# Queries and keys with both halves of the input side by side, and two value weight splits moved to the head of the norm

## The chip, the cores and the metric

The kernel runs on one core of one Trainium2 chip. The metric is the device time of one execution in microseconds (us). Times of several runs are given as their median. One execution was taken with the hardware profiler; its rows are what the prediction is read from.

## The reference

Two blocks of a transformer work on 256 tokens of width 1024. The change lies in the first block's attention layer and in the normalization ahead of it:

```python
h = modulate(rmsnorm(x, norm_mix[1]), sh1, sc1)
qkv = h @ w_qkv                     # (256, 1024) @ (1024, 3072)
q, k, v = split(qkv, 3)             # 16 heads of 64
logits = q @ k.T * 64**-0.5 + bias  # causal, one block of 256 keys
o = softmax(logits) @ v
x = x + g1 * (o @ w_o)
```

Ahead of it stands the first MLP (`relu(h @ w_up)**2 @ w_down`, width 4096), behind it the second MLP of the block, and then a second block with a gated delta rule, a forgetting attention and a gated MLP.

## The kernel before

All inputs are 32-bit floats, and TensorE takes each operand as a high part and a low part (32-bit floats of reduced precision): a product is the sum of three matmuls, high by high, low by high and high by low (`mm3`). Weights come from DRAM in loads of 1 MB (128 x 2048), issued on SP's queue into three raw buffers. Each load holds two pieces of 1024 columns. A piece is split when it is first asked for (`Chunk.piece`): ScalarE writes the high part (L248), VectorE subtracts it from the raw weights for the low part (L254). Five buffers hold the high parts of pieces, five the low parts.

The down projection of the MLP (`rows_steps`, tiles `dn`) sums into four banks, one for each half of the tokens (t) and of the columns (n). Its last chunk ends with token half 0; the matmuls of token half 1 are held back and handed to the next boundary. Ahead of the last chunk `prefetch` asks for the first pieces of the next weights, here four pieces of the value weights (`wv`).

A boundary (`boundary`) adds the sums to x (`add`: times the gate, L547, then to x, L548), squares and sums each row on ScalarE (L346), works out the row's factor (L354 to L323), normalizes (`xn`; VectorE L595 the first 512 columns, ScalarE L596 the rest), transposes on PE (L599), scales and shifts on ScalarE (`hf`, L392) and splits the result into high and low on VectorE (L398, L399). Inside a boundary the instructions of PE, VectorE and ScalarE keep the order in which they are written; `products(n)` puts n steps of the held matmuls, and then of the first products of the next layer, between them. The branch taken ahead of attention is the last one (`else`): seven steps, the transposes of half 0, one step, four, two, the transposes of half 1, two. The same branch is taken by the boundary "f" ahead of the last MLP. Outside a boundary a list scheduler orders what each engine does, after the order of the program, the buffers and its own estimate of times.

Attention takes the values of the first 512 columns (tiles `v`), and then the projections of q and k (tiles `qk`), in an order on PE that is written out: for each half of the heads, q and k of four heads, then q and k of the next four (`project`, two tiles of 128 rows by 256 tokens in each call; 16 tiles in all). Scores, transposes of the probabilities and their products with the values are put between the steps by a table of due times; each projection step counts 0.64 there. The projections use the two banks of the kind `mm`, and so do the value tiles. `ride` puts leftover work of other layers (column sums `wmc`, L473, on VectorE) behind a projection; it may start after the instruction of VectorE named in `ride_after`.

The MLP of the second layer and the gated MLP of the second block keep the high and the low part of their input side by side in one buffer (`hl_beside`), so that one matmul of 512 columns streams both over the high weights (L1010), and one of 256 streams the high part over the low weights (L1011); ScalarE copies one half of the bank (L1017) and VectorE adds the other (L1018). They use four banks, `mm` and `tp` in turn (`halves_tile`).

Of the kernel before, what the change touches and what calls it, by code (L numbers as in the profile page):

```python
# [12 lines left out]
ALU = mybir.AluOpType  # L13

P = 128
# [121 lines left out]
def costing(gen, cost):  # L137

    for _ in gen:
        yield cost  # L140
# [20 lines left out]
def build(tc, a, out):  # L161
# [4 lines left out]
    with ctx:  # L166
# [13 lines left out]
        def mm_tile(name):  # L180
            return pmm.tile([P, 512], F32, tag="mm", name=name)
# [16 lines left out]
        def last_on(engine):  # L198
            return next(i for i in reversed(nc.cur_bb.bb.instructions) if i.engine == engine)
# [81 lines left out]
        def vcol(v):  # L281
            return vecs[:, v * KT:(v + 1) * KT]
# [139 lines left out]
        def hl_tiles(name, n):  # L422
            hi = big_tile(f"{name}_hi", F32R)[:, :KT * n].rearrange("p (k n) -> p k n", k=KT)
            lo = big_tile(f"{name}_lo", F32R)[:, :KT * n].rearrange("p (k n) -> p k n", k=KT)
            return hi, lo
# [128 lines left out]
        def boundary(ac, gate, scale, shift, h, c0, name, ahead, final=None):  # L554
# [3 lines left out]
            with tc.manual_schedule(engines=VA | {mybir.EngineType.PE}):  # L558
# [9 lines left out]
                def add(t, n):  # L568
                    c = slice(n * 512, (n + 1) * 512)
                    add_to_x(ac[t, n], t, n, gate, None, f"{name}{t}{n}")  # L570
                    if final is not None:
                        vec.tensor_tensor(src[t][:, c], x[:, t, c], final[:, c], ALU.mult)
# [34 lines left out]
                def products(n):  # L607
                    for _ in range(n):
                        next(ahead[0], None)

                add(0, 0)
                squares(0, 0)
                add(0, 1)
                squares(0, 1)
                w = ahead[1]
                if final is not None:
                    products(R_REST + 1)
                    normalize(0)
                    products(5)
                    w.piece_hi(3)  # L620
                    add(1, 0)
                    hfs = [scaled(0, kt) for kt in (0, 2)]
                    squares(1, 0)
                    add(1, 1)
                    squares(1, 1)
                    split(hfs[0], 0, 0)
                    split(hfs[1], 0, 2)
                    hfs = [scaled(0, kt) for kt in (4, 6)]
                    products(4)

                    def beside():
                        w.piece_lo(3)
                        products(2)

                    normalize(1, beside)
                    split(hfs[0], 0, 4)
                    split(hfs[1], 0, 6)
                    products(4)
                elif w is not None:
                    products(R_HOLD)  # L640
                    w.piece_hi(2)
                    normalize(0)
                    products(8 - R_HOLD)
                    w.piece_lo(2)
                    for kt in range(0, KT, 2):
                        split(scaled(0, kt), 0, kt)
                    w.piece_hi(3)
                    add(1, 0)
                    squares(1, 0)
                    add(1, 1)  # L650
                    squares(1, 1)
                    w.piece_lo(3)
                    products(6)
                    normalize(1)
                    products(2)
                else:
                    products(R_REST - 1)
                    normalize(0)
                    products(1)
                    add(1, 0)  # L660
                    hfs = [scaled(0, kt) for kt in (0, 2)]
                    squares(1, 0)
                    split(hfs[0], 0, 0)
                    split(hfs[1], 0, 2)
                    products(4)
                    add(1, 1)
                    hfs = [scaled(0, kt) for kt in (4, 6)]
                    squares(1, 1)
                    split(hfs[0], 0, 4)
                    products(2)  # L670
                    normalize(1, lambda: split(hfs[1], 0, 6))
                    products(2)
# [320 lines left out]
        def ws_steps(w, h, ft, ps, c0=0, n=S, grain=4):  # L993

            for kt in range(KT):
                mm3(ps, w(ft * PIECE + kt * P, P), hl(h, kt, slice(c0, c0 + n)), kt == 0, kt == KT - 1)
                if (kt + 1) % grain == 0:
                    yield
# [3 lines left out]
                pass  # L1002

        def ws_halves(w, h, ft, ps):


            p2 = ps.rearrange("p (e n) -> p e n", e=2)
            for kt in range(KT):
                wl = w(ft * PIECE + kt * P, P)
                pe.matmul(p2, wl[0], both(h, kt, slice(0, S)), start=kt == 0, stop=False)  # L1010
                pe.matmul(p2[:, 0], wl[1], h[0][:, kt], start=False, stop=kt == KT - 1)  # L1011

        def halves_tile(q, name):
            return (mm_tile, tp_tile)[q](name)
# [63 lines left out]
        def prefetch(w, n=4):  # L1078
            def go():
                for i in range(n):  # L1080
                    w.piece(i)
            return go

        def mlp(i, h, w0, wn, at, ahead=None):
# [73 lines left out]
            def chunk(j):  # L1158
                at(j)
                nxt = max(j + 1, len(acts)) if j != 1 or i else 0  # L1160
                if nxt < 8 and nxt not in acts:
# [2 lines left out]

            return drain(rows_steps(8, chunk, lambda j, k, t: (acts[j][:, 0, k, t * P:(t + 1) * P],
                                                               acts[j][:, 1, k, t * P:(t + 1) * P]),
                                    f"dn{i}", prefetch(wn, (4, 3)[i]), hold=True))


        def softmax_rows(ps, bias, n, name, p=None):  # L1170
# [30 lines left out]
        def attention(i, h, w0, wn):  # L1201
# [31 lines left out]

            def project(w, half, which, pr):
                dst, sc = ((qT, 0.125), (kT, 1.0))[which]
                ps = mm_tile(f"qk{which}{half}{pr}")
                for q in range(2):
                    yield from costing(ws_steps(w, h, 2 * pr + q, ps[:, q * S:(q + 1) * S], grain=2), 0.64)
                kt = 4 * half + 2 * pr
                o4 = dst[:, kt:kt + 2].rearrange("p k (t n) -> p (k t) n", t=2)  # L1240
                p4 = ps.rearrange("p (a n) -> p a n", n=P)
                ride_after[:] = [last_on(mybir.EngineType.DVE)]
                act.activation(o4, p4[:, :, ::-1] if which == 0 else p4, AF.Copy, scale=sc)
                riding()

            def riding():
# [151 lines left out]

        wv0 = split_chunk(a["w_v"][0], "wv0")
        ac, rest = mlp(0, mlp0_h, None, wv0, lambda j: rel_bias_vector() if j == 1 else None, wu02)  # L1400
        h = hl_tiles("att1", S)
        firsts = []

        def ahead(rest, w, h, name):
# [2 lines left out]
            firsts.append(mm_tile(name))  # L1407
            yield from tm_steps(w, h, 0, P, firsts[-1], 1)

        boundary(ac, lambda: gates[0, 1], *mods(1, 0), h, 0, "att1", (ahead(rest, wv0, h, "v00"), None))  # L1410
        wu1 = Chunk(a["w_up0"], "wu10", inmraw=2)
        ac, rest = attention(1, h, wv0, wu1)
        while len(pending) > 4:
            ride(4)
        h = hl_beside("mlp1", S)
        boundary(ac, lambda: gates[1, 0], *mods(1, 1), h, 0, "mlp1", (ahead(rest, wu1, h, "up100"), wu1))

        def wide_row(src, name):
            row = big_tile(name)[:, :D]
# [33 lines left out]
            yield from meta  # L1453
            yield from first

        boundary(ac, lambda: gates[1, 1], vcol(V_ATT), None, u, NMETA, "u", (second_ahead(), wfv), early["nf"])
        p1ctx.close()
        p2 = ctx.enter_context(tc.tile_pool(name="p2", bufs=1, reuse_waits="tile"))
        masks = p2.tile([P, M_N], F32, name="masks")
# [580 lines left out]
        ac, rest = drain(wo)  # L2040

        fh = hl_beside("f", S)
        boundary(ac, None, vcol(V_FFN), None, fh, 0, "f", (ahead(rest, wg0, fh, "gu00"), None))
        NJ = DFF2 // 256

        def fa_tile(j):
# [160 lines left out]
```

## Time and profile before

| | |
|---|---|
| time, median of 3 runs | 926.99 us (925.73 to 929.45) |
| time of the profiled execution | 926.48 us |
| its span, first to last instruction | 924.7 us |
| PE busy | 902.5 us, 98% |
| VectorE (DVE) busy | 664.6 us, 72% |
| ScalarE (ACT) busy | 521.1 us, 56% |
| mean granted TensorE clock | 0.995 of full speed |

The span is shorter than the time by what lies before the first and behind the last instruction. Busy times are sums over the whole span; an engine with 72% can be full in one stage and half idle in another. Matmuls overlap, so the length of one says less than the distance from one start to the next.

### The profile page before, as it was taken

The page shows a single profiled execution, that of the slowest core. Times are in us where ns is not written, and L with a number is a line of the kernel's source. Part 1 is how long each engine was busy: PE and PEld are TensorE (multiplying, and loading weights), DVE is VectorE, ACT ScalarE, POOL GpSimd, SP SyncE. Part 2 cuts the span into 40 slices and gives each one's busy share as a digit, 9 for nine tenths or more (in the row PEclk, how much of TensorE's full clock was granted, in tenths as well). Part 3 has the DMA queues.
Part 4 walks back from the last instruction along what each step waited for, and adds up shares of the span by engine and source line. Part 5 has one row for each costly group of instructions (what it writes and reads, how often), then busy time and mean ns, then how long its engine had stood idle before and what let it go on. Part 6 is the DMA issues. An engine that isn't in the chain of part 4 may idle for free.

```text
span 924.7 us, 14385 instructions
## 1 busy us (share of the span) xinstructions
PE 902.5 (98%) x5501; PEld 763.3 (83%) x5501; DVE 664.6 (72%) x1296; ACT 521.1 (56%) x957; POOL 12.7 (1%) x22
## 2 busy tenths in 40 slices
PE   7999999999899999999999999999999999999996
PEld 3668889999799987888888878999988788888885
DVE  1686889998698785896566678797458775666554
ACT  4466544445467764665555656766456555545552
POOL 0000000000000000000000001000000000000000
PEclk9999999999999999999999999999999999999998
DMA  9998879999477561875565634432113565555531
GB/s 363 420 421 325 302 279 373 378 342 354 139 252 285 171 229 42 295 277 183 190 219 181 241 110 173 138 110 75 46 47 98 199 204 204 184 182 183 186 134 45
DMA packets 34552, 198.25 MB, mean 214 GB/s; under 512 B 4186, under 2 KB 6818, under 8 KB 14002
## 3 DMA queue, kind: packets, MB, share of 16 engines
q1 hardware_dynamic: 34338, 197.27, 59.5%
q8 instruction: 43, 0.70, 0.3%
q14 instruction: 25, 0.20, 0.1%
q10 hardware_dynamic: 146, 0.08, 0.0%
HBM read 196.24 MB, written 1.09 MB: 213 GB/s over the span
## 4 chain that ended last, share of the span: by engine, by line
PE 88%; DVE 4%; DMA 3%; issue 2%; ACT 1%; SPq 0%; POOL 0%; DVEq 0%; POOLq 0%; ACTq 0%
PE gu L1010 8%; PE dn L265 6%; PE dn L266 6%; PE dn L267 6%; PE up L1010 6%; PE gu L1011 4%; PE qk L294 4%; PE up L265 4%; PE up L267 4%; PE up L266 3%; PE up L1011 3%; DMA wms<-in_w_mods_dram 2%; PE fd L265 2%; PE fd L267 2%; PE fd L266 2%
## 5 line engine op out<-in xcount | busy, mean ns | idle before, releaser
L1010 PE MATMUL gu<-f,wgu_h 128*128 128x512 f32 x320 | 113.5, 398 | 0.0
L248 ACT ACTIVATE wd_h<-wd_r 128x1024 fp32r<-128x1024 f32 x58 | 61.2, 1061 | 73.9 <-PE up L1010 27.1
L254 DVE TENSOR_TENSOR wd_l<-wd_r,wd_h 128x1024 fp32r<-128x1024 f32 x58 | 70.7, 1224 | 34.8 <-ACT wd_h L248 34.6
L266 PE MATMUL dn<-wd_l,a 128*128 128x512 f32 x232 | 90.6, 390 | 0.0
L265 PE MATMUL dn<-wd_h,a 128*128 128x512 f32 x232 | 90.5, 391 | 0.0
L267 PE MATMUL dn<-wd_h,a 128*128 128x512 f32 x232 | 90.1, 390 | 0.0
L1011 PE MATMUL gu<-f,wgu_l 128*128 128x256 f32 x320 | 89.8, 281 | 0.0
L254 DVE TENSOR_TENSOR wu_l<-wu_r,wu_h 128x1024 fp32r<-128x1024 f32 x58 | 70.0, 1222 | 23.7 <-ACT wu_h L248 23.6
L248 ACT ACTIVATE wu_h<-wu_r 128x1024 fp32r<-128x1024 f32 x58 | 60.7, 1062 | 43.2 <-PE dn L267 36.6
L1010 PE MATMUL up<-mlp,wu_h 128*128 128x512 f32 x224 | 79.3, 397 | 0.0
L254 DVE TENSOR_TENSOR wgu_l<-wgu_r,wgu_h 128x1024 fp32r<-128x1024 f32 x44 | 53.6, 1225 | 35.0 <-ACT wgu_h L248 35.0
L248 ACT ACTIVATE wgu_h<-wgu_r 128x1024 fp32r<-128x1024 f32 x44 | 46.7, 1063 | 48.5 <-issue 22.8
L1010 PEld LDWEIGHTS gu<-f,wgu_h 128*128 128x128 f32 x320 | 60.1, 188 | 14.7
L1011 PE MATMUL up<-mlp,wu_l 128*128 128x256 f32 x224 | 62.9, 281 | 0.0
L1011 PEld LDWEIGHTS gu<-f,wgu_l 128*128 128x128 f32 x320 | 60.4, 189 | 0.4
L267 PE MATMUL up<-mlp_hi,wu_l 128*128 128x256 f32 x192 | 54.3, 284 | 0.6 <-DVE wu_l L254 0.6
L265 PE MATMUL up<-mlp_hi,wu_h 128*128 128x256 f32 x192 | 54.4, 283 | 0.0
L266 PE MATMUL up<-mlp_lo,wu_h 128*128 128x256 f32 x192 | 54.3, 283 | 0.0
L266 PEld LDWEIGHTS dn<-wd_l,a 128*128 128x128 f32 x232 | 43.6, 188 | 9.3 <-issue 0.6
L265 PEld LDWEIGHTS dn<-wd_h,a 128*128 128x128 f32 x232 | 43.6, 188 | 9.0
L267 PEld LDWEIGHTS dn<-wd_h,a 128*128 128x128 f32 x232 | 43.4, 188 | 9.2
L1010 PEld LDWEIGHTS up<-mlp,wu_h 128*128 128x128 f32 x224 | 42.0, 188 | 10.0
(868 smaller groups left out, 2393.0 us busy)
## 6 DMA issues: line engine op xcount, KB each, us to landing
wu_r<-in_w_up_dram SPq DMA_DIRECT2D x32, 1024.0 KB, 6.4
wd_r<-in_w_down_dram SPq DMA_DIRECT2D x32, 1024.0 KB, 5.8
wgu_r<-in_w_gu_dram SPq DMA_DIRECT2D x22, 1024.0 KB, 5.2
wmc<-in_w_modc_dram SPq DMA_DIRECT2D x16, 1024.0 KB, 7.0
wmg<-in_w_modg_dram SPq DMA_DIRECT2D x12, 1024.0 KB, 7.6
wfd_r<-in_w_fd_dram SPq DMA_DIRECT2D x11, 1024.0 KB, 4.9
wi_r<-in_w_in_dram SPq DMA_DIRECT2D x10, 1024.0 KB, 5.2
wms<-in_w_mods_dram SPq DMA_DIRECT2D x16, 512.0 KB, 9.9
```

The lines of the kernel that those rows point to most:

```text
L248: act.activation(hi, r, AF.Copy)
L254: vec.tensor_tensor(lo, r, hi.bitcast(F32), ALU.subtract)
L265: pe.matmul(ps, l[0], r[0], start=first, stop=False)
L266: pe.matmul(ps, l[0], r[1], start=False, stop=False)
L267: pe.matmul(ps, l[1], r[0], start=False, stop=last)
L294: f(*a, **k)
L1010: pe.matmul(p2, wl[0], both(h, kt, slice(0, S)), start=kt == 0, stop=False)
L1011: pe.matmul(p2[:, 0], wl[1], h[0][:, kt], start=False, stop=kt == KT - 1)
```

## The change

The input of attention, `h`, is laid out side by side (`hl_beside` in place of `hl_tiles`). `project` takes one whole bank for each of its tiles: for each of eight k-steps a matmul of 512 columns (high and low of the input, over the high weights) and one of 256 (the high part, over the low weights, added to the first half of the bank), in place of three of 256. A yield is added to the function that does this, so that other work can go between its steps as before. To take a tile out, ScalarE copies the second half, scaled, into a buffer of the kind `t2k`, and VectorE multiplies the first half by the scale and adds the copy, into q or k. There are 16 such pairs in place of 8 copies of two tiles each. `ride_after` is set once a call, ahead of the second tile's copy.

`prefetch` at the end of the first MLP asks for two value pieces in place of four. The other two (2 and 3) are asked for at the head of the boundary, ahead of the first addition, where the written order holds; the load that feeds them is asked for there too. A third entry of `ahead` carries this; the other boundaries give an empty one, and take the branches that they took.

```diff
+                w, early = ahead[1:]
+                for i in early:
+                    w.piece(i)
                 add(0, 0)
                 squares(0, 0)
                 add(0, 1)
                 squares(0, 1)
-                w = ahead[1]
...
-                elif w is not None:
+                elif not early and w is not None:
...
         def ws_halves(w, h, ft, ps):
+            for _ in halves_steps(w, h, ft, ps):
+                pass
+
+        def halves_steps(w, h, ft, ps):
...
                 pe.matmul(p2, wl[0], both(h, kt, slice(0, S)), start=kt == 0, stop=False)
                 pe.matmul(p2[:, 0], wl[1], h[0][:, kt], start=False, stop=kt == KT - 1)
+                if kt % 2:
+                    yield
...
-                                    f"dn{i}", prefetch(wn, (4, 3)[i]), hold=True))
+                                    f"dn{i}", prefetch(wn, (2, 3)[i]), hold=True))
...
                 dst, sc = ((qT, 0.125), (kT, 1.0))[which]
-                ps = mm_tile(f"qk{which}{half}{pr}")
                 for q in range(2):
-                    yield from costing(ws_steps(w, h, 2 * pr + q, ps[:, q * S:(q + 1) * S], grain=2), 0.64)
-                kt = 4 * half + 2 * pr
-                o4 = dst[:, kt:kt + 2].rearrange("p k (t n) -> p (k t) n", t=2)
-                p4 = ps.rearrange("p (a n) -> p a n", n=P)
-                ride_after[:] = [last_on(mybir.EngineType.DVE)]
-                act.activation(o4, p4[:, :, ::-1] if which == 0 else p4, AF.Copy, scale=sc)
+                    ps = mm_tile(f"qk{which}{half}{pr}{q}")
+                    yield from costing(halves_steps(w, h, 2 * pr + q, ps), 0.64)
+                    o2 = dst[:, 4 * half + 2 * pr + q].rearrange("p (t n) -> p t n", t=2)
+                    p4 = ps.rearrange("p (a n) -> p a n", n=P)
+                    if which == 0:
+                        p4 = p4[:, :, ::-1]
+                    if q:
+                        ride_after[:] = [last_on(mybir.EngineType.DVE)]
+                    low = t2k(f"qk{which}{half}{pr}{q}l")[:, :S].rearrange("p (t n) -> p t n", t=2)
+                    act.activation(low, p4[:, 2:], AF.Copy, scale=sc)
+                    vec.scalar_tensor_tensor(o2, p4[:, :2], sc, low, ALU.mult, ALU.add)
                 riding()
...
-        h = hl_tiles("att1", S)
+        h = hl_beside("att1", S)
...
-        boundary(ac, lambda: gates[0, 1], *mods(1, 0), h, 0, "att1", (ahead(rest, wv0, h, "v00"), None))
+        boundary(ac, lambda: gates[0, 1], *mods(1, 0), h, 0, "att1", (ahead(rest, wv0, h, "v00"), wv0, (2, 3)))
```

## Rows read from the trace of the kernel before

**Rows 1.** The page: busy time of each engine, and the chain that ended last.

```profile
PE 902.5 (98%) x5501; PEld 763.3 (83%) x5501; DVE 664.6 (72%) x1296; ACT 521.1 (56%) x957; POOL 12.7 (1%) x22
...
PE 88%; DVE 4%; DMA 3%; issue 2%; ACT 1%; SPq 0%; POOL 0%; DVEq 0%; POOLq 0%; ACTq 0%
```

**Rows 2.** Busy time by stage (start:end, length; then each engine, clock, DMA).

```profile
244.00:260.00 16.00, 13.42 (x65) 10.79 (x66) 12.51 (x32) 12.29 (x27) 1.02 (x2) 1.00 0.13 54
260.00:274.00 14.00, 13.92 (x115) 13.60 (x116) 14.00 (x20) 7.35 (x9) 0.00 (x0) 1.00 0.93 335
274.00:286.00 12.00, 12.00 (x103) 11.20 (x100) 9.71 (x41) 8.36 (x22) 0.00 (x0) 1.00 0.95 341
...
311.00:326.00 15.00, 15.00 (x129) 13.77 (x128) 12.86 (x33) 10.65 (x22) 0.00 (x0) 1.00 0.50 165
326.00:342.00 16.00, 15.87 (x113) 13.15 (x111) 15.41 (x49) 12.76 (x29) 0.00 (x0) 1.00 0.71 257
```

**Rows 3.** Timeline of PE at the boundary (start, length; in brackets idle and releaser).

```profile
243.48 0.39 PE L267 MATMUL dn<-wd_p,a 128*128 128x512 f32 x1
...
245.49 1.09 PE L599 MATMUL att_tp<-ident,att_xn 128*128 128x128 f32 x8 [1.63 <-DVE att_xn L595]
...
247.47 0.47 PE L265 MATMUL v<-wv_h,att_hi 128*128 128x512 f32 x1 [0.18 <-DVE att_hi L398]
...
252.74 1.06 PE L599 MATMUL att_tp<-ident,att_xn 128*128 128x128 f32 x8 [0.91 <-DVE att_xn L595]
```

**Rows 4.** Timeline of DVE at the same boundary.

```profile
238.01 0.69 DVE L547 TENSOR_TENSOR att_t<-dn,gate 128x512 f32<-128x512 f32 x1 [4.78 <-PE dn L267]
...
238.62 1.22 DVE L254 TENSOR_TENSOR wv_l<-wv_r,wv_h 128x1024 fp32r<-128x1024 f32 x1
...
240.95 1.22 DVE L254 TENSOR_TENSOR wv_l<-wv_r,wv_h 128x1024 fp32r<-128x1024 f32 x1
...
244.95 0.49 DVE L595 TENSOR_SCALAR att_xn<-x,att_y 128x512 f32<-128x512 f32 x1
```

**Rows 5.** Timeline of ACT before it.

```profile
233.12 2.01 ACT L248 ACTIVATE wv_h<-wv_r 128x1024 fp32r<-128x1024 f32 x2 [1.33 <-DMA wv_r<-in_w_v_dram]
```

**Rows 6.** Timeline of PE where the later boundary of the same form stands.

```profile
728.70 1.03 PE L599 MATMUL f_tp<-ident,f_xn 128*128 128x128 f32 x8
...
734.94 1.06 PE L599 MATMUL f_tp<-ident,f_xn 128*128 128x128 f32 x8 [0.22 <-DVE f_xn L595]
```

**Rows 7.** Timeline of PE: where the first and the fifth projection tile begin.

```profile
260.49 0.28 PE L294 MATMUL qk<-att_hi,wqk_h 128*128 128x256 f32 x1
...
272.00 0.28 PE L294 MATMUL qk<-att_hi,wqk_h 128*128 128x256 f32 x1
```

**Rows 8.** Timeline of PE in the gate stage: fourteen pairs, first and next after them.

```profile
799.79 0.40 PE L1010 MATMUL gu<-f,wgu_h 128*128 128x512 f32 x1
...
804.74 0.40 PE L265 MATMUL fd<-wfd_h,fa 128*128 128x512 f32 x1
```

**Rows 9.** Timeline of ACT: evacuations of q, and of a side-by-side tile of the MLP.

```profile
266.32 1.06 ACT L248 ACTIVATE wqk_h<-wqk_r 128x1024 fp32r<-128x1024 f32 x1 [1.82 <-PE qk L294]
...
267.29 0.58 ACT L1243 ACTIVATE att_q<-qk 128x512 f32<-128x512 f32 x1
...
402.06 1.06 ACT L248 ACTIVATE wd_h<-wd_r 128x1024 fp32r<-128x1024 f32 x1 [1.63 <-PE up L1010]
...
403.02 0.37 ACT L1017 ACTIVATE up120s<-up 128x256 f32<-128x256 f32 x1
```

**Rows 10.** Timeline of PE and DVE: that MLP tile's last matmul and its sum.

```profile
401.86 0.28 PE L1011 MATMUL up<-mlp,wu_l 128*128 128x256 f32 x1
...
405.32 0.42 DVE L1018 TENSOR_TENSOR up120s<-up,up120s 128x256 f32<-128x256 f32 x1
```

**Rows 11.** Timeline of DVE and of PE's weight loads at attention's end.

```profile
326.05 0.42 DVE L1033 TENSOR_TENSOR att_o_lo<-pv,att_o_hi 128x256 fp32r<-128x256 f32 x1 [0.42 <-ACT att_o_hi L1032]
...
337.10 0.46 PEld L294 LDWEIGHTS pt<-ident,sm 128*128 128x128 f32 x3 [0.37 <-DVE sm L1183]
```

More of the change, by code (lines that the diff above doesn't have):

```diff
@@ L1415, in build @@
         h = hl_beside("mlp1", S)
-        boundary(ac, lambda: gates[1, 0], *mods(1, 1), h, 0, "mlp1", (ahead(rest, wu1, h, "up100"), wu1))
+        boundary(ac, lambda: gates[1, 0], *mods(1, 1), h, 0, "mlp1", (ahead(rest, wu1, h, "up100"), wu1, ()))
         def wide_row(src, name):
@@ L1454, in second_ahead @@
             yield from first
-        boundary(ac, lambda: gates[1, 1], vcol(V_ATT), None, u, NMETA, "u", (second_ahead(), wfv), early["nf"])
+        boundary(ac, lambda: gates[1, 1], vcol(V_ATT), None, u, NMETA, "u", (second_ahead(), wfv, ()), early["nf"])
         p1ctx.close()
@@ L2042, in build @@
         fh = hl_beside("f", S)
-        boundary(ac, None, vcol(V_FFN), None, fh, 0, "f", (ahead(rest, wg0, fh, "gu00"), None))
+        boundary(ac, None, vcol(V_FFN), None, fh, 0, "f", (ahead(rest, wg0, fh, "gu00"), None, ()))
         NJ = DFF2 // 256
```

## The prediction

> **What bounds the kernel now.** I read the page first: TensorE is busy 98% of the span and makes up 88% of the chain that ended last [rows 1]. So a microsecond is won only where PE stands idle or where its stream gets shorter, and lost wherever PE is made to wait. Next I read the stages around the edit [rows 2], to see where PE idles and how full VectorE is, because the edit gives VectorE new work. PE misses 2.6 us of the 16 us at the boundary before attention, and almost nothing in the stages after it. VectorE is full in the first projections (14.00 of 14 us), has gaps in the next stage (9.71 of 12) and is close to full at the end of attention (12.86 of 15, then 15.41 of 16). Then the timelines, for the waits behind these sums.
>
> At the boundary PE ends the seven held products with the matmul of 243.48 and stands 1.63 us before the first transposes; it waits 0.18 us at the first value product and 0.91 us at the second transposes [rows 3]. The release of the first is the normalized row half at 244.95, and in front of it on VectorE two weight splits of 1.22 us each stand between the additions, while VectorE had been idle for 4.78 us before the first addition [rows 4]. The weight halves that these splits need were made on ScalarE from 233.12 on, as soon as the load had landed [rows 5]. So the splits could run in the idle time ahead.
>
> **The splits and the boundary.** The two splits are moved, with their two ScalarE conversions and the one load that feeds them; nothing is added. The load keeps its place on SP's queue: no other load is issued between the old point and the new one, and the projection weights still follow it. ScalarE converts at 233.1 to 235.1, VectorE subtracts behind it and is done near 236.4, and the first addition starts at 238.0 as before, since it waits for PE. What waits behind the splits on VectorE, now in a fixed order, is that addition; the cover is 1.6 us, and beyond it a later load costs 1 us for 1 us. The normalized half then comes up to 2 x 1.22 = 2.4 us earlier. PE can use only its 1.63 us of idle time, because the seven held products end when they did; they are what is late next. The second wait stays: from the first transposes to the second, VectorE and ScalarE run the same chain (scale, split, add, square), which no edit shortens. The later boundary that takes the same branch and the same side-by-side layout has the first transposes without any wait and 0.22 us at the second [rows 6], so the layout itself costs nothing there. Term: -1.63 us; bounds 0 (load late) and -2.7 (all three waits go).
>
> **The stream.** A projection tile has 8 k-steps. Before, each is three matmuls over 256 columns: four tiles take 272.00 - 260.49 = 11.51 us, 2.88 us a tile [rows 7]. After, each is one matmul over 512 columns and one over 256, the pair that the gate stage runs: 14 pairs take 804.74 - 799.79 = 4.95 us, so 0.354 us a pair and 2.83 us a tile [rows 8]. One weight load in three goes too, but loads overlap the matmuls in both rows. 16 tiles x 0.05 = -0.8 us. The number of columns is the same, and only what an extra matmul costs is saved; one can be misled by the durations (398 + 281 against 3 x 283 ns), since matmuls overlap.
> The Trainium skill (TensorE: Matmul & The Clock Gate, "Wait — 56ns, not 53.3ns?") gives a warm matmul N / 2.4 GHz plus about 2.5 ns from start to start. By it one matmul less a step is worth 2.5 ns, an estimate of 128 x 2.5 ns = 0.3 us, where the rows give 0.8; the rows decide, and no other number here rests on it.
>
> **The evacuation.** Before, two tiles share one bank and one ScalarE copy of 0.58 us takes both out [rows 9]. After, each tile fills a bank (high products in one half, low ones in the other): 16 copies of 0.37 us on ScalarE (1.3 us more in all, in stages where it is half idle), and 16 sums on VectorE. The trace has no such fused sum on PSUM; the nearest row is the MLP's sum of two halves, 0.42 us [rows 10], so about 6.7 us of new VectorE work. Two prices follow.
>
> First, banks. The projections have two banks. Before, a bank had to be free 5.8 us after its pair ended; after, 2.83 us after its tile ended. At best the copy waits behind the weight conversion that the same tile end releases (1.06 us, as at 266.32), and copy and sum follow: 1.06 + 0.37 + 0.42 = 1.85 us, no stall. At worst it goes as in the MLP, with VectorE full of other splits: its tile ends at 401.86 + 0.28 = 402.14, its sum at 405.32 + 0.42 = 405.74, 3.60 us [rows 9, 10]. The MLP has four banks and does not feel it; here it would be 3.60 - 2.83 = 0.77 us for each tile while VectorE is full, the first four: 3.1 us. Later tiles have the scores, transposes and value products of attention between them (12 tiles from 272.0 to about 326.5, less some 8 us for a value quarter, 3.9 us a tile), more than 3.60. Taking a lag anywhere between 1.85 and 3.60 as equally likely, the mean stall is 0.77 x 0.77 / 2 / 1.75 = 0.17 us, over four tiles 0.7 us. Term: +0.7, bounds 0 and 3.1.
>
> Second, the end of attention. From the fifth pair's scores (about 316) VectorE runs nearly without a gap until PE's transposes at 337.10, which wait for its softmax product; the one gap is 0.42 us at 326.05 [rows 11]. Three or four of the new sums fall in there. Three at 0.42 less the gap: +0.8 us; bounds 0 (the scheduler finds them other gaps) and 4 x 0.42 = 1.7.
>
> At nothing I cost: the earlier start of the first scores' input (the first tile of a pair is now copied alone), the new buffers for the low halves (eight of that kind, some five held by scores and probabilities at a time, by the code's order), and everything behind the edited stage, where PE's work is the same.
>
> **Sum.** -1.63 - 0.78 + 0.7 + 0.8 = -0.9 us. The profiled execution took 926.48 us (span 924.7), so 925.6; the median of the three runs, 926.99, is 0.5 above it, so I name 926.1. The tellable difference is 0.5%, 4.6 us: no change that can be told.
>
> **Rivals.** (a) All of the gain stays: the sums find gaps, no bank is late. -2.4 us, 924.6. For it: VectorE's gaps in the middle stages; against: 15.41 of 16 at the end. Still no change that can be told. (b) The splits are not early after all: the load, asked for later in the program, comes over 1.6 us later, and the additions wait behind it. The 1.63 goes: 927.7, or more if the load is far late. Against it: the load's queue is not otherwise used between the two points. (c) It ends slower: the two banks couple PE to VectorE's queue at every tile. If all 16 tiles pay 0.77 us, that is 12.3 - 2.4 + 0.8 = +10.7 us, 937.7. It decides from (4.6 + 1.6) / 16 = 0.39 us a tile. For it: the MLP's 3.60 us lag with the same two operations; against: the wider spacing of the later tiles.
> The Trainium skill (Perfetto Trace Analysis, "Identifying Performance Opportunities") says that the same gap repeating on the engine that should be saturated can mean too few buffers for the next tile; that is how (c) would look, and no row of this trace shows it. (d) Faster by over 0.5%: the waits of the boundary and the stream together are 1.63 + 0.18 + 0.91 + 0.78 = 3.5 us, less than 4.6, so it takes a luckier order elsewhere.
>
> **Numbers.** Forecast (-2 to +1.5) 0.55; (a) 0.17; (b) 0.10; (c) 0.12; (d) 0.06. All but (c) and (d) lie within 0.5%, and a part of (c) too, while (b) can be worse: faster 0.06, same 0.81, slower 0.13. The lower end takes every wait that can go, 926.5 - 3.5, so 923.0; the upper end takes both prices at their bounds and no gain at the boundary, 926.99 + 3.1 + 1.7 - 0.8 = 931.0.
>
> **What would show it.** Right: the two splits end before the first addition, the first transposes follow the held products with no wait, pairs start 0.354 us apart, the sums take 0.42 us. Wrong: PE idle at the head of projection tiles, ended by VectorE; an idle gap before the transposes near 335 much over 0.8 us; a first addition behind a late split.

## The result, and the profile after

The changed kernel takes 934.78 us (median of 5 runs, 933.45 to 935.19), against 928.42 us for the kernel before (5 runs). The ratio is 1.0077, with a 95% interval of 1.0059 to 1.0094: slower, by more than the 0.5% that can be told. The forecast was 926.1 us, between 923.0 and 931.0, and no change, so it was wrong. The profiled execution has a span of 933.0 us, 8.3 us more than the 924.7 of before. The first boundary and the stream did what was forecast; the loss lies in the attention.

The page still shows TensorE as the bound, at 97% against 98% [rows 1]:

```profile
PE 904.0 (97%) x5373; PEld 758.1 (81%) x5373; DVE 669.5 (72%) x1312; ACT 522.0 (56%) x965; POOL 12.7 (1%) x22
```

Such an average does not say where 8 us went. The windows by stage do (length, then busy time of PE, PEld, DVE, ACT, POOL with the number of instructions, then PE's granted clock, DMA share, GB/s), behind them the last stage as it was before:

```profile
244.00:260.00 16.00, 14.92 (x74) 12.02 (x73) 12.86 (x30) 13.21 (x28) 0.55 (x1) 1.00 0.05 9
260.00:274.00 14.00, 10.52 (x51) 8.83 (x50) 12.37 (x21) 4.48 (x7) 0.00 (x0) 0.88 0.99 376
274.00:286.00 12.00, 12.00 (x74) 9.60 (x73) 9.77 (x34) 7.05 (x15) 0.00 (x0) 1.00 0.70 222
286.00:301.00 15.00, 12.72 (x71) 10.04 (x70) 11.05 (x43) 8.63 (x24) 0.00 (x0) 0.89 0.66 217
```

```profile
286.00:300.00 14.00, 14.00 (x119) 12.31 (x119) 11.58 (x40) 9.34 (x21) 0.00 (x0) 1.00 0.73 258
```

The boundary is better than before: PE misses 1.1 us in 16 where it missed 2.6 [rows 2]. But two stages that were full now miss 3.5 and 2.3 us, and in these two the granted clock is below 1. The timeline of PE shows the boundary first, then the heads of projection tiles, that is, their first matmuls (in brackets: idle, and what ended it):

```profile
243.57 0.39 PE L267 MATMUL dn<-wd_p,a 128*128 128x512 f32 x1
243.80 1.03 PE L599 MATMUL att_tp<-ident,att_xn 128*128 128x128 f32 x8
...
250.99 1.06 PE L599 MATMUL att_tp<-ident,att_xn 128*128 128x128 f32 x8 [0.90 <-DVE att_xn L595]
...
258.74 0.39 PE L294 MATMUL qk<-att,wqk_h 128*128 128x512 f32 x1
...
261.43 0.28 PE L294 MATMUL qk<-att,wqk_l 128*128 128x256 f32 x1
261.55 0.40 PE L294 MATMUL qk<-att,wqk_h 128*128 128x512 f32 x1
...
268.02 0.50 PE L294 MATMUL qk<-att,wqk_h 128*128 128x512 f32 x1 [3.48 <-DVE att_q L1255]
...
291.51 0.50 PE L294 MATMUL qk<-att,wqk_h 128*128 128x512 f32 x1 [2.28 <-DVE att_k L1255]
...
330.66 0.50 PE L294 MATMUL qk<-att,wqk_h 128*128 128x512 f32 x1 [1.25 <-DVE att_q L1255]
...
346.15 0.70 PE L294 MATMUL pt<-ident,sm 128*128 128x128 f32 x3 [0.95 <-DVE sm L1191]
```

The first transposes follow the held products without the 1.63 us of [rows 3]; the second keep their wait. A tile takes 261.55 - 258.74 = 2.81 us. Then three heads of tiles wait for VectorE's sum (line 1255), 7.0 us together. Why the first sum is so late is read in VectorE's timeline, which is the order of its queue, with the ScalarE copy that the sum needs in a fence of its own behind it:

```profile
262.80 1.27 DVE L473 CUSTOM_DVE_ANT_0 wmc<-wmc,crow,vecs 128x1024 f32<-128x1024 f32 x1
...
264.01 1.27 DVE L473 CUSTOM_DVE_ANT_0 wmc<-wmc,crow,vecs 128x1024 f32<-128x1024 f32 x1
...
265.29 2.34 DVE L254 TENSOR_TENSOR wqk_l<-wqk_r,wqk_h 128x1024 fp32r<-128x1024 f32 x2
267.56 0.41 DVE L1255 SCALAR_TENSOR_TENSOR att_q<-qk,qk0000l 128x256 f32<-128x256 f32 x1
```

```profile
262.60 0.36 ACT L1254 ACTIVATE qk0000l<-qk 128x256 f32<-128x256 f32 x1
```

The tile ended at 261.43 + 0.28 = 261.71 and its copy at 262.96. The sum could have run then, and ended at 267.97: 6.3 us after its tile. VectorE was not waiting for anything; it ended two earlier splits (the last 1.1 us of the 6.3), then did one riding pair of column sums (wmc, 2.5 us) and two more weight splits (2.3 us), all of which stand in front. The next tile covers 2.83 of the 6.3 us and PE stands for the rest. In the other two cases a riding pair stands in front of the sum as well (at 288.63 and 289.83, at 325.42 and 326.62), in the last case with softmax work and a split behind it.

After two of these waits PE is slow too. This is a part of its timeline after the first:

```profile
269.29 0.63 PE L294 MATMUL qk<-att,wqk_h 128*128 128x512 f32 x1
269.72 0.41 PE L294 MATMUL qk<-att,wqk_l 128*128 128x256 f32 x1
269.93 0.63 PE L294 MATMUL qk<-att,wqk_h 128*128 128x512 f32 x1
...
272.48 0.40 PE L294 MATMUL qk<-att,wqk_h 128*128 128x512 f32 x1
```

The pairs are 0.64 us apart instead of 0.354 [rows 8]: the clock has fallen to its 1.2 GHz level, from 269.1 to 272.4. Five pairs cost 5 x 0.29 = 1.4 us. After the wait of 2.28 us the same goes on from 293.06 to 296.39, where four pairs and three transposes take 3.3 us instead of some 1.7: 1.6 us. After the wait of 1.25 us no matmul is slow.

The account of the change is then: boundary -1.6, stream 16 x (2.88 - 2.81) = -1.1, heads of tiles +7.0, low clock +3.0, end of attention +0.95, in sum +8.2 us, against +8.3 in the spans. From the last held product ahead of attention to the first transposes of the next boundary, the trace gives +8.5 us (113.28 to 121.79 us). The stream's share takes the first tile's 2.81 us for all sixteen.

### The profile page after: what moved, and what is told of

It reads as the page before. It is cut to its first block, busy times and chain, and to the rows that moved or that the text cites. A ratio compares the mean times of both kernels' runs of the same rounds, so it can differ in the third digit from the quotient of the medians.

```text
span 933.0 us, 14152 instructions
## 1 busy us (share of the span) xinstructions
PE 904.0 (97%) x5373; PEld 758.1 (81%) x5373; DVE 669.5 (72%) x1312; ACT 522.0 (56%) x965; POOL 12.7 (1%) x22
## 3 DMA queue, kind: packets, MB, share of 16 engines
HBM read 196.24 MB, written 1.09 MB: 212 GB/s over the span
## 4 chain that ended last, share of the span: by engine, by line
PE 88%; DVE 5%; DMA 3%; issue 2%; ACT 1%; SPq 0%; POOL 0%; DVEq 0%; POOLq 0%; ACTq 0%
PE gu L1016 8%; PE dn L266 6%; PE dn L265 6%; PE dn L267 6%; PE up L1016 6%; PE gu L1017 4%; PE qk L294 4%; PE up L265 3%; PE up L267 3%; PE up L266 3%; PE up L1017 3%; DMA wms<-in_w_mods_dram 2%; PE fd L265 2%; PE fd L267 2%; PE fd L266 2%
## 5 line engine op out<-in xcount | busy, mean ns | idle before, releaser
L294 PE MATMUL qk<-att,wqk_h 128*128 128x512 f32 x128 | 50.3, 428 | 7.0 <-DVE att_q L1255 4.7
```

The source lines that it names most:

```text
L294: f(*a, **k)
```

## The experiments

All ratios are to the kernel before, on the same chip and in the same session. Edits are shown against the changed kernel unless said otherwise; "..." marks lines left out.

**The early splits alone.** The block of the projections is put back as it was; the splits ahead of the additions and the side-by-side input stay.

```
+                ps = mm_tile(f"qk{which}{half}{pr}")
                 for q in range(2):
-                    ps = mm_tile(f"qk{which}{half}{pr}{q}")
-                    yield from costing(halves_steps(w, h, 2 * pr + q, ps), 0.64)
...
+                    yield from costing(ws_steps(w, h, 2 * pr + q, ps[:, q * S:(q + 1) * S], grain=2), 0.64)
...
+                act.activation(o4, p4[:, :, ::-1] if which == 0 else p4, AF.Copy, scale=sc)
```

> The boundary part without the projections: two value pieces split at the head of the norm, input side by side, but projections as before (three matmuls of 256 columns, two tiles a bank, one copy). Theory (two banks coupled to VectorE's queue cost the time, the boundary is a gain): 1.6 to 1.8 us faster than before, ratio 0.998, PE's 1.63 us wait before the first transposes gone. Rival (the early splits or the new layout cost something behind the boundary): not faster, ratio 1.000 or more.

Measured: 925.06 us, ratio 0.9973 (0.9959 to 0.9987), 2.5 us faster. PE's waits from 235 to 350 us (total, times, longest):

```profile
PE att_tp L599 <- DVE att_xn L595: 0.9, 1, 0.9
PE v L265 <- DVE att L398: 0.2, 1, 0.2
```

The wait of 1.6 us of [rows 3] is gone and nothing takes its place.

**The new projections alone.** The projections as changed, the splits back between the additions.

```
-                                    f"dn{i}", prefetch(wn, (2, 3)[i]), hold=True))
+                                    f"dn{i}", prefetch(wn, (4, 3)[i]), hold=True))
...
-        boundary(ac, lambda: gates[0, 1], *mods(1, 0), h, 0, "att1", (ahead(rest, wv0, h, "v00"), wv0, (2, 3)))
+        boundary(ac, lambda: gates[0, 1], *mods(1, 0), h, 0, "att1", (ahead(rest, wv0, h, "v00"), None, ()))
```

> The projections without the early splits: side by side, one bank a tile, VectorE's sums, but four value pieces prefetched as before. Theory: the whole loss is here, 8 to 10 us slower than before, ratio 1.009 to 1.011, with PE waiting for VectorE's sums at the head of two or three projection tiles. Rival (the loss comes of PE arriving earlier at a VectorE that is no earlier): under 5 us slower, ratio 1.005 or less, since PE is as late here as before.

Measured: 939.09 us, ratio 1.0129 (1.0107 to 1.0152), 12 us slower. PE's waits in the same stretch, then the window after the first of them (columns as above):

```profile
PE qk L294 <- DVE att_q L1255: 5.9, 3, 3.5
PE att_tp L599 <- DVE att_xn L595: 2.5, 2, 1.6
PE qk L294 <- DVE att_k L1255: 2.3, 1, 2.3
PE pt L294 <- DVE sm L1191: 1.0, 1, 1.0
...
```

```profile
270.00:275.00 5.00, 4.66 (x17) 4.03 (x18) 4.30 (x9) 0.12 (x1) 0.00 (x0) 0.66 0.96 372
```

The two parts of the change are separate: one wins some 2.5 us, the other loses 12 alone, and some 10 beside the first (ratio 1.0077 against 0.9973). The loss alone is somewhat more than the theory's 8 to 10 us, and the rival, under 5 us, is out.

**ScalarE frees the bank.** ScalarE copies the whole bank (512 columns), and VectorE adds the halves from the copy, so no bank waits for VectorE.

```
-                    act.activation(low, p4[:, 2:], AF.Copy, scale=sc)
-                    vec.scalar_tensor_tensor(o2, p4[:, :2], sc, low, ALU.mult, ALU.add)
...
+                    act.activation(both2, ps, AF.Copy, scale=sc)
...
+                    vec.tensor_tensor(o2, b4[:, :2], b4[:, 2:], ALU.add)
```

> The changed kernel, but ScalarE copies the whole bank (512 columns) and VectorE adds the two halves from the copy, so a bank is free when ScalarE is done. VectorE's sums and their places in its queue stay. Theory (it is the bank that waits for the sum): no wait of PE at the head of a projection tile, the granted clock stays at full speed, 1 to 3 us faster than before, ratio 0.997 to 0.999. Rival (VectorE has too much work in this stage, whoever holds the bank): the wait moves to the scores, which need q and k, and 4 us or more of the loss stay, ratio 1.004 or more.

Measured: 926.96 us, ratio 1.0008 (0.9991 to 1.0025): the loss is gone, but the gain of 1 to 3 us that the theory named is not shown. No head of a tile waits and the clock stays at 1.00, but two other waits are there:

```profile
PE s L294 <- DVE att_k L1258: 1.9, 1, 1.9
PE pt L294 <- DVE sm L1191: 1.7, 1, 1.7
```

**Four banks.** The tiles of a pair go to two kinds of bank: the first to the two of the kind `mm`, the second to the four of the kind `acc`, which the transposes and value products use too. So a bank comes round after four tiles at the earliest instead of two. The sums stay in VectorE's queue.

```
-                    ps = mm_tile(f"qk{which}{half}{pr}{q}")
+                    ps = (mm_tile, acc_tile)[q](f"qk{which}{half}{pr}{q}")
```

> The changed kernel, but the second tile of each projection call takes a bank of the kind with four buffers, so a bank is asked for again only after four tiles or more. Theory (two banks are too few for a sum that comes 6 us late): waits at the heads of tiles gone, 1 to 3 us faster than before, ratio 0.997 to 0.999. Rival (too much work on VectorE): the sums are as late as in the changed kernel and PE waits at the scores, ratio 1.004 or more.

Measured: 926.61 us, ratio 1.0004 (0.9987 to 1.0021). Again no wait at a head, clock 1.00, and the same two waits (second fence: the first sum in VectorE's timeline):

```profile
PE s L294 <- DVE att_k L1255: 1.8, 1, 1.8
PE pt L294 <- DVE sm L1191: 1.7, 1, 1.7
```

```profile
265.96 0.43 DVE L1255 SCALAR_TENSOR_TENSOR att_q<-qk,qk0000l 128x256 f32<-128x256 f32 x1
```

With the sums as late as in the changed kernel (the first ends at 266.39, 6.3 us after its tile at 260.14, in front of it the same riding pair and splits), the additional banks take away all 7 us of waits and the slow clock. What these two kernels do not show is a gain: they stay 3 us behind the early splits alone, with 3.5 us of waits that the latter does not have: PE's scores reach k's sum too early (1.8 us), and the last transposes wait for the softmax (1.7 us). The Trainium skill (Perfetto Trace Analysis, "Matmuls") says that independent groups of matmuls should rotate through different PSUM banks so that the evacuation of one overlaps the next; the traces of the two kernels agree, with 7.0 us of waits at two banks and none at four.

**The riding pairs behind the sum, two banks.** The mark from which the riding pair may follow is set after the second sum of a pair of tiles instead of ahead of it.

```
-                    if q:
-                        ride_after[:] = [last_on(mybir.EngineType.DVE)]
...
                     vec.scalar_tensor_tensor(o2, p4[:, :2], sc, low, ALU.mult, ALU.add)
+                ride_after[:] = [last_on(mybir.EngineType.DVE)]
```

> The changed kernel whole, still with two banks for the projections' tiles; only the column-sum pairs that ride on the stream (the two wmc operations of 1.2 to 1.3 us each) are now put into VectorE's queue behind the second sum of a pair of tiles instead of ahead of it. Theory (two banks wait for sums that stand late in VectorE's in-order queue): at the first waiting head two low-part splits are left in front of the sum, so 3.5 us become about 1.0, and the waits of 2.3 and 1.25 us go, since 2.4 us of work is gone from in front of each; the granted clock does not fall; with 2.5 us of slow matmuls saved as well, the ratio to the kernel before is 0.998 to 1.002. Rival (the splits, and not the order, set the lag; the queue is as long either way): the waits move by less than 1 us together and the ratio stays at 1.006 to 1.009.

Measured: 933.1 us, ratio 1.007 (1.0053 to 1.0086). The expected time was not reached; it is the rival's, though not for the rival's reason. The heads' waits did shrink: the one that waited 3.48 us no longer waits, three others do with 0.85, 1.68 and 0.60 us, 3.1 in sum against 7.0. But the last transposes wait 3.43 us, and the clock falls after that (second fence, columns as above):

```profile
PE pt L294 <- DVE sm_nm L1188: 3.4, 1, 3.4
PE qk L294 <- DVE sm_nm L1188: 1.7, 1, 1.7
...
PE qk L294 <- DVE att_k L1253: 0.8, 1, 0.8
PE qk L294 <- DVE att_q L1253: 0.6, 1, 0.6
```

```profile
340.00:350.00 10.00, 8.48 (x33) 6.36 (x34) 5.91 (x28) 4.96 (x15) 0.00 (x0) 0.66 0.96 371
```

So here the order of the queue decides which wait appears, and the work put later falls on what is later.

**Both: four banks, riding pairs behind the sum.** The two edits above together.

> Four banks for the projections' tiles and the riding pairs behind the sums. Theory: no wait at any tile's head, and the scores' wait of 1.8 us for k's sum, which stood behind a riding pair, is gone or under 0.5 us; what is left of the loss is the wait of the last transposes for VectorE's softmax, 1.7 us: ratio 0.997 to 0.9995. Rival (VectorE is late by its whole load, whatever the order): the scores and the last transposes wait 3 us or more together as with four banks alone, ratio 1.000 to 1.002.

Measured: 933.15 us, ratio 1.0063 (1.0044 to 1.0082). The waits of the heads and of the scores are gone, but the transposes wait for the softmax, once in the middle and once at the end, and the clock is at 0.66 from 340 to 350 us here too. Both theories missed: neither had the pair's 2.5 us come back in front of the softmax.

```profile
PE pt L294 <- DVE sm L1191: 5.9, 2, 3.8
```

**Sums that nobody reads.** The early splits alone, and after each pair of tiles two additions of 128x256 on VectorE without a reader (shown against the early splits alone).

```
                 act.activation(o4, p4[:, :, ::-1] if which == 0 else p4, AF.Copy, scale=sc)
+                for q in range(2):
+                    low = t2k(f"qk{which}{half}{pr}{q}l")[:, :S].rearrange("p (t n) -> p t n", t=2)
+                    o2 = dst[:, kt + q].rearrange("p (t n) -> p t n", t=2)
+                    vec.scalar_tensor_tensor(low, o2, sc, o2, ALU.mult, ALU.add)
```

> The early splits alone, with the projections as in the kernel before, and after each pair of tiles two additions of 128x256 on VectorE whose results nobody reads (16 in all, some 0.35 to 0.42 us each, 6 to 7 us together). It prices the load of VectorE without any wait for a bank or for a sum. Theory (the end of the attention pays for VectorE's added work): a wait of 1.0 to 1.7 us of the last transposes for the softmax appears that is not there without them; ratio 0.998 to 0.9995, against 0.997 for the early splits alone. Rival (VectorE has slack, and only waits for banks and sums cost): ratio 0.9965 to 0.9975, and no such wait.

Measured: 926.21 us, ratio 1.0 (0.9987 to 1.0013). The additions take 0.42 to 0.43 us each, 6.8 us in all, and PE's transposes wait where they did not:

```profile
PE pt L294 <- DVE sm L1191: 1.9, 2, 1.5
...
PE pt L294 <- DVE sm_nm L1188: 0.3, 1, 0.3
```

VectorE's load alone, without a bank or a sum that anyone waits for, costs 2.2 us of waits, close to what the ratio says beside the early splits alone (1.0 against 0.9973, 2.5 us). VectorE is busy 72% of the span, but 10.00 of 10 us in this kernel from 320 to 330 and from 330 to 340.

**The sums on GpSimd.** ScalarE copies the whole bank, GpSimd adds the halves (shown against the kernel in which ScalarE frees the bank).

```
-                    vec.tensor_tensor(o2, b4[:, :2], b4[:, 2:], ALU.add)
+                    pool.tensor_tensor(o2, b4[:, :2], b4[:, 2:], ALU.add)
```

> The changed kernel, but ScalarE copies the whole bank (512 columns) to SBUF and GpSimd, not VectorE, adds the halves from the copy. VectorE's queue is that of the kernel before. Theory (all of the loss lies in VectorE's queue and in its load): no wait at a tile's head, none of the last transposes, the scores wait for k's sum under 0.7 us; the boundary's 2.5 us and some of the stream's 0.8 are kept: ratio 0.996 to 0.9975. Rival (the projections in this form cost elsewhere too, in ScalarE's longer copies or in an addition on GpSimd of 1.5 us or more that the scores wait for): 0.998 to 1.001.

Measured: 924.37 us, ratio 0.9973 (0.996 to 0.9986). It is the only version of the new projections with all its work that beats the kernel before, and by as much as the early splits alone; the two intervals do not part them. No head and no scores wait; the last transposes wait 0.8 us, which was not expected. Some of VectorE's operations are longer beside GpSimd's additions. Two groups in this run, from 259 to 345 us (count, busy us, mean ns, idle before):

```profile
L473 DVE CUSTOM_DVE_ANT_0 wmc<-wmc,crow,vecs 128x1024 f32<-128x1024 f32 x12 | 16.5, 1410 | 0.0
L1191 DVE TENSOR_SCALAR sm<-sm,sm_rs 128x256 f32<-128x256 f32 x16 | 6.8, 425 | 0.2
```

and with the early splits alone, where GpSimd does nothing in this stretch:

```profile
L473 DVE CUSTOM_DVE_ANT_0 wmc<-wmc,crow,vecs 128x1024 f32<-128x1024 f32 x12 | 14.9, 1280 | 0.0
...
L1191 DVE TENSOR_SCALAR sm<-sm,sm_rs 128x256 f32<-128x256 f32 x16 | 5.6, 352 | 0.2
```

**Short riding operations, two banks.** The twelve column sums in the attention work on 128 of 1024 columns, which leaves most of that sum out of the later norms. One takes 346 instead of 1281 ns, so VectorE has 11 us less to do.

```
-            vec.tensor_tensor_reduce(out=w, in0=w, in1=crow, ...)
+            n = 128 if short[0] else D
+            vec.tensor_tensor_reduce(out=w[:, :n], in0=w[:, :n], in1=crow[:, :n], ...)
...
+        short[0] = True
         ac, rest = attention(1, h, wv0, wu1)
+        short[0] = False
```

> The changed kernel whole, with its two banks, but the twelve wmc operations that ride in VectorE's queue during the attention work on 128 of their 1024 columns, which leaves most of the column sums of the later norms out: VectorE has some 13 us less to do in the attention, with the order of its queue unchanged. Theory (VectorE's load in the attention sets both how late a sum stands and how late the last softmax is): the first waiting head is left with about 1.0 us, the two others and the wait of the last transposes are gone, the granted clock stays at its upper level; ratio to the kernel before 0.9965 to 0.9985. Rival (two banks couple TensorE to the sums whatever the load): two or more heads wait over 1 us each, ratio 1.002 or more.

Measured: 925.9 us, ratio 0.9986 (0.9975 to 0.9996). The wait of 3.48 us is gone altogether (the first sum starts at 264.71 instead of 267.56), 2.1 us are left in three later heads, none at the end, and the clock stays at 1.00 through the attention. A little less was gained than the theory said at the heads, and it was the first, not the others, that went to nothing.

**Short riding operations, four banks.** The edits of "Four banks" and of the run above together.

> Four banks for the projections' tiles and the twelve short wmc operations. Theory: no wait at any tile's head, scores wait under 0.7 us, none of the last transposes; the boundary's 2.5 us and the stream's forecast 0.8 both stay: ratio 0.9955 to 0.997. Rival (the projections in this form gain nothing in the stream): 0.997 to 0.998, no better than the early splits alone.

Measured: 922.98 us, ratio 0.9958 (0.9944 to 0.9971). From 235 to 350 us PE waits nowhere but at the boundary, with 0.9 and 0.2 us. This bounds what the new projections could be worth if VectorE had room; work is left out here.

**Short riding operations, early splits alone.** The control: the old projections, the early splits and the short operations.

> The early splits alone, with the projections of the kernel before, and the twelve short wmc operations: the control for the two runs above. Theory: TensorE waited for VectorE nowhere in this attention, so 13 us less of work on VectorE change nothing: ratio 0.9965 to 0.998, as the early splits alone. Rival (VectorE's load costs this form too): 0.9955 or less.

Measured: 926.23 us, ratio 0.9991 (0.9978 to 1.0004), not the 0.9965 to 0.998 of the theory and away from the rival too. The transposes wait 0.9 us and a value product 0.4 us that did not wait with the full operations. The interval overlaps that of the early splits alone; whether less work on VectorE does harm here is left open. Just before the transposes' wait VectorE itself stands 1.56 us until ScalarE has converted a weight (to 331.38), so that wait is at least not VectorE's load alone. In the same session the new projections with four banks are 926.23 - 922.98 = 3.25 us faster than this control, of which 1.3 us are the control's own two waits.

**The riding pairs in the middle, four banks.** No work is left out; the pairs ride behind other steps.

```
-RIDES = (1, 2, 3, 6, 8, 10)
+RIDES = (3, 4, 5, 6, 7, 8)
```

> Four banks for the projections' tiles, all work kept, and the six riding pairs moved to other places of the attention: behind its steps 3 to 8 instead of 1, 2, 3, 6, 8 and 10, so that none stands in VectorE's queue before the first sums and none close to its end. Theory (a sum or a softmax is late by what stands in front of it in the queue, and VectorE has room in the middle, 7 to 8 of 10 us busy from 295 to 320 us): the scores' wait of 1.8 us goes, that of the last transposes shrinks to under 0.8 us; ratio to the kernel before 0.9955 to 0.998. Rival (the whole load is too much wherever it stands): waits of 2.5 us or more remain in the attention, ratio 0.999 or more.

Measured: 929.57 us, ratio 1.0036 (1.0021 to 1.005). The wait at the end is gone, as the theory said, and that of the scores shrank from 1.8 to 0.8 us where the theory had it go. But two pairs now stand together in front of a softmax in the middle (294.21 to 299.5, the first of them 1.40 us late because its load is), the transposes wait 4.0 us for it, and the clock falls again. The time is the rival's, and so is a wait of over 2.5 us.

```profile
PE pt L294 <- DVE sm L1191: 4.0, 1, 4.0
...
PE s L294 <- DVE att_k L1255: 0.8, 1, 0.8
```

```profile
300.00:310.00 10.00, 6.00 (x33) 5.35 (x32) 8.83 (x34) 3.78 (x12) 0.00 (x0) 0.83 0.48 166
```

**The same with two banks.**

> The same move of the riding pairs with the changed kernel's two banks. Theory: the wait of 3.5 us at the first waiting head falls to about 1, since the pair that stood in front of the first sum is gone; but each pair that moved to the middle can still make a head wait there, by the 1 to 2.5 us that it holds VectorE; ratio 0.998 to 1.004. Rival (the two banks cost what they cost whatever rides where): 1.006 or more.

Measured: 937.68 us, ratio 1.0132 (1.0111 to 1.0152), the rival's time and not the theory's. The first head still waits, 2.21 us, and five more do. The theory had no pair in front of the first sum; in the trace one stands there (263.77 and 264.98).

```profile
PE qk L294 <- DVE att_k L1255: 4.5, 2, 2.3
PE qk L294 <- DVE att_q L1255: 3.9, 3, 2.2
PE qk L294 <- DVE sm_nm L1188: 1.2, 1, 1.2
```

No place of the six pairs that was tried is free of a wait with two banks; with four, the places that the kernel had are the best of three.

## Why the prediction was wrong

**The splits and the boundary: right.** The forecast was -1.63 us, and the first transposes lost their wait of 1.63 us and no other; the early splits alone give -2.5 (interval -1.2 to -3.8). The second wait stays at 0.90 us [rows 3]. The cover of 1.6 us was nearly used up: the second conversion on ScalarE starts at 234.53, 1.4 us later than in [rows 5], because its load lands later, and the splits end at 237.98, just before the addition at 238.10. Rival (b) was that close: in the run of the early splits alone the addition starts right behind the splits too (239.42), in that of the sums that nobody reads 1.81 us of idle time lie between, as the loads took 8.0 us at most to land in the changed kernel and 6.3 us in that run.

**The stream: right.** 2.81 us for the first tile against the 2.83 of the forecast, -1.1 us instead of -0.8 if all sixteen run so.

**The banks: the step that failed.** The term was +0.7 with a bound of 3.1 for four tiles; the heads measured +7.0, and one of them alone 3.48. Two assumptions of it were wrong. The lag of a sum was taken from the MLP's row, 3.60 us at worst [rows 10], as if VectorE's queue held only splits here; it also holds the riding pairs, which [rows 2] counted as busy time but which no row of the sum put in front of a tile. The rest of two splits, one pair and two more splits, then the sum itself, made 6.3 us. And the later tiles were let off because they are 3.9 us apart on average, while a head waits for one sum in one place of the queue: two of the three waits are among those tiles. More banks, and ScalarE as the only reader of the bank, each take all of it away, so it is shown that the waits come from two banks held by late sums. Rival (c) had the mechanism, a tile held by VectorE's queue, but not its form: three long waits instead of sixteen of 0.77 us.

**The clock: not in the sum at all.** After two of the waits the granted clock fell to its 1.2 GHz level, +3.0 us more. The longest stall of a tile in the prediction was 0.77 us, so it never asked what a longer one does to the clock.

**The end of attention: right in mechanism, its size in part luck.** +0.8 forecast, 0.95 measured in the changed kernel, but there PE had lost some 10 us on the way; 1.7, the upper bound, where no wait at a head delays PE. Idle additions alone bring 2.2 us of waits, so VectorE's load is enough to make such a wait.

**The input of the scores: costed at nothing, and wrong.** It was said to come earlier, since the first tile of a pair is copied alone. It comes later, since it now ends with VectorE's sum instead of ScalarE's copy: 1.8 us where nothing else makes PE late. In the changed kernel the longer waits hide it.

The new projections thus gain some 1.1 us on PE, and their 6.7 us of sums fall on the one queue that had little room for them. Whether the last 3 us at four banks are due to the order of the queue or to its load was not fully parted. The order matters (other places of the pairs move the waits by up to 4 us), the load too (with four banks, short pairs remove them all), and no order that was tried removes them at full load.

Of the versions with all their work, the early splits with the old projections (925.06 us, ratio 0.9973) and the sums on GpSimd (924.37 us, 0.9973) beat both kernels, the kernel before by 0.3% with intervals clear of 1. The first is the simpler one and would be kept.

## What to carry to other kernels

When an evacuation moves to an engine that works through its queue in order, as VectorE does in these traces, price its lag by all that can stand in front of it in that queue at that place, background work first, and set it against the time in which the banks come round; an average spacing or another stage's lag does not bound it. A bank should be read by the engine with the shortest queue, or there must be enough banks to outlast the longest stretch in front of the reader. Where the engine is full for 20 us on end, moving its background work may only choose which wait appears, as in the three places tried here.

## What was not expected of the hardware

The granted clock fell to its 1.2 GHz level after some waits of TensorE of 2.2 to 4.0 us, and the length of a wait alone does not tell after which. It fell after 3.48 and 2.28 us in the changed kernel (1.4 and 1.6 us more), after 3.50 with the new projections alone, after 3.43 and 3.75 with the riding pairs behind the sum (0.66 from 340 to 350 us in both) and after 4.00 with four banks and the pairs in the middle. It did not fall after the waits of up to 1.87 us at this boundary and in this attention. In between it went either way: in the last run it fell after one wait of 2.21 us and after one of 2.29 and stayed up after another of 2.21, and it stayed up after 2.19 us with four banks and the pairs behind the sum, and after 2.28 us with the new projections alone (1.00 from 295 to 300 us).

VectorE slowed beside GpSimd. With sixteen additions of 128x256 on GpSimd, VectorE's column sums took 1410 instead of 1280 ns on average and the softmax's product of 128x256 425 instead of 352, while the softmax's first operation, which reads PSUM, stayed at 416 against 422. In the kernel where ScalarE copies the same whole banks but VectorE adds, the first two stay at 1281 and 352, so it is GpSimd's work and not ScalarE's. The averages hide the form: of the twelve column sums eight keep their length (1.27 or 1.28 us), and the four that start while GpSimd is adding end 1.08 or 1.09 us after that addition, as in these two cases (GpSimd's line, then VectorE's):

```profile
263.60 1.44 POOL L1258 TENSOR_TENSOR att_q<-qk0000l 128x256 f32<-128x256 f32 x1 [13.48 <-ACT qk0000l L1254]
264.37 1.75 DVE L473 CUSTOM_DVE_ANT_0 wmc<-wmc,crow,vecs 128x1024 f32<-128x1024 f32 x1
...
269.26 1.55 POOL L1258 TENSOR_TENSOR att_k<-qk1000l 128x256 f32<-128x256 f32 x1 [1.33 <-ACT qk1000l L1254]
270.14 1.75 DVE L473 CUSTOM_DVE_ANT_0 wmc<-wmc,crow,vecs 128x1024 f32<-128x1024 f32 x1
```

The additions end at 265.04 and 270.81, the column sums at 266.12 and 271.89. GpSimd's additions vary as well, from 0.73 us, where VectorE reads PSUM beside them (275.97), to 1.81. The Trainium skill (SBUF — State Buffer, "SBUF: two separate sides") says that the two engines share one pair of SBUF ports, which one holds for a whole instruction while the other is blocked, and that a VectorE operation with two SBUF inputs or in a two-port mode is among those that need it. The trace agrees: a column sum, with its two inputs in SBUF, is 0.47 us longer (1.75 us against 1.28) where it meets an addition, and the operation with an input in PSUM is no longer than without GpSimd.
